# A decoder layer's SwiGLU "down" product in two groups of 4 and 7 chunks instead of three groups

## The chip, the cores and the metric

The kernel runs on one core of one Trainium2 chip. The metric is device time in microseconds (us) of one execution; 1763.42 us is the median of three runs of the kernel before (1762.24 to 1764.12).

## The reference, cut to what matters

One decoder layer for 256 tokens of width 2048, all in float32: a SwiGLU feed-forward block, a token mixer (latent attention and sparse attention side by side), a second SwiGLU block, each followed by a residual sum and a layer norm. Only the two feed-forward blocks are touched:

```
def swiglu(x, w_gate, w_up, w_down):
    return (jax.nn.silu(x @ w_gate) * (x @ w_up)) @ w_down
...
        x = layer_norm(DEEPNORM_ALPHA * x + FFN_RES_WEIGHT * swiglu(x, ffn1_w_gate[l], ffn1_w_up[l], ffn1_w_down[l]),
                       ln1_g[l], ln1_b[l])
...
        x = layer_norm(DEEPNORM_ALPHA * x + FFN_RES_WEIGHT * swiglu(x, ffn2_w_gate[l], ffn2_w_up[l], ffn2_w_down[l]),
                       ln3_g[l], ln3_b[l])
```

`w_gate` and `w_up` are 2048 x 5632, `w_down` is 5632 x 2048. The 5632 hidden columns are 11 *chunks* of 512.

## The kernel before, in words

**Products in three parts.** Each float32 operand is split into a rounded part and a remainder (`split`, L90: a cast on ScalarE, L91, then a subtraction on VectorE, L92), and each block product is three matmuls of 512 columns (`mm3`, L94: L96, L97, L98). L97 is the one that needs the remainder of the weights, `wlo`, which VectorE makes last.

**Units.** `gemm2` (L251) computes two column tiles of 512 (a *column pair*) for both token tiles at once. It walks over *units*: two row tiles of the weight (2 x 128 rows) by two column tiles. An ordinary unit is 8 block products, 24 matmuls, and two loaded buffers to split. A *seven-product unit* (Strassen-Winograd) is 7 block products, 21 matmuls. For it VectorE also forms sums of weights (L318 of 1024 columns, L319 and L320 of 512), and four buffers are split: `a` (1024 columns), `b` (512), and the sums `t13` and `t24` (1024 each). It also needs sums of the left operand, which `trans` (L455) or `sums` (L386) make earlier. While sevens run, four PSUM banks hold outputs and four hold shared products. After the last seven of a column pair the four shared products are combined (ScalarE copy L357, VectorE L358 to L361), and at the end of the pair each of the four output banks gets its combination added (L370) and is handed to `fin`, which for "down" adds it to the residual `y` (L526 for the first group, L528 later). For the last group `done` follows: layer norm statistics of that piece (`ln_stats`, L561), and when a token tile is whole, its layer norm.

**Buffers.** Loaded weights go through 5 buffers (`rawp`), weight sums through 3 (`sump`), the split parts through 6 pairs (`hip`, `lop`). Where a product has no sevens, loads alternate between `rawp` and `sump` by a counter (`new_raw`, L143).

**Order of the work.** TensorE and the DMA queue of SyncE run in program order as written. VectorE and ScalarE instructions are put in an order when the program is built, and that order is fixed: an instruction that stands behind a waiting one is issued after it. Transposes of the hidden activations are generators (`trans`, spawned at L504 and L516) that are stepped by `tick`, each time a given count of products later; `held` keeps them out of the sevens, where all 8 banks are in use.

**The feed-forward block** (`ffn`, L448) goes: gate and up of chunks 0-1 and 2-3, gate 4-5, **down of group 0** (chunks 0 to 3), up 4-5, gate and up 6-7, gate 8-9, **down of group 1** (chunks 4 to 7), up 8-9, gate and up of chunk 10 (`last`, L506), **down of group 2** (chunks 8 to 10). Groups 0 and 1 are 8 units per column pair, 4 of them sevens. Group 2 is 6 units with 2 sevens for the first column pair; the second column pair has no sevens and runs through `gemm` (L177), one column tile after the other, the last with `tail=6`: all products of token tile 0 first, then those of token tile 1, so that the layer norm of tile 0 runs beside tile 1. In all 4+4, 4+4 and 2 sevens: 18 per block.

## Time and profile before

| what | value |
|---|---|
| median of three runs | 1763.42 us (1762.24 to 1764.12) |
| profiled execution, first to last instruction | 1761.7 us |
| TensorE (PE) busy, 8058 matmuls | 1741.7 us, 99% |
| VectorE (DVE) busy | 1596.9 us, 91% |
| ScalarE (ACT) busy | 993.9 us, 56% |
| mean granted TensorE clock | 0.998 |

The profiled execution's own device time is not listed apart from the three runs; its span is 1.7 us below their median.

How to read the profile: a busy time is that of one engine, and engines overlap. The time shown for one matmul (some 390 ns) includes its way through the array, and matmuls overlap in it, so what a matmul costs is the distance from start to start. The same holds in smaller measure on VectorE: the chain of waits, which counts each instant once, gives what an instruction costs behind another one. Ln is line n of the kernel before.

### The profile page before, as it was taken

How to read it: one execution, taken by the hardware profiler on the slowest of the kernel's cores; microseconds unless marked ns; L12 is line 12 of the kernel's file. 1: busy time of each engine (PE TensorE's matmuls, PEld its weight loads, DVE VectorE, ACT ScalarE, POOL GpSimd, SP SyncE). 2: the span in 40 equal slices, each digit the busy share in tenths (PEclk: the TensorE clock that was granted, in tenths of full speed). 3: DMA queues.
4: the chain of work that ended last, by engine and by line, in shares of the span. 5: the costliest groups of instructions: out<-in, count | busy, mean ns of one | idle time of the engine just before them, and what ended most of it. 6: DMA issues, size and time to landing. Idle time of an engine off the chain costs nothing.

```text
span 1761.7 us, 22427 instructions
## 1 busy us (share of the span) xinstructions
PE 1741.7 (99%) x8058; PEld 1429.6 (81%) x8058; DVE 1596.9 (91%) x2123; ACT 993.9 (56%) x1306; POOL 17.0 (1%) x39
## 2 busy tenths in 40 slices
PE   9999999999999999999999999999999999999997
PEld 7888888888888888887788778888888878878886
DVE  7899999999999998765587679999999999999997
ACT  6656555574655565654455556565655565655651
POOL 0000000000000000000000000000000000000000
PEclk9999999999999999999999999999999999999999
DMA  9665666556656657545853355655566556556654
GB/s 334 218 211 178 204 204 203 191 184 212 197 196 225 204 172 255 181 139 206 283 195 111 132 168 179 203 179 203 192 206 222 201 181 215 191 193 217 203 200 159
DMA packets 103408, 350.01 MB, mean 199 GB/s; under 512 B 11136, under 2 KB 13696, under 8 KB 103296
## 3 DMA queue, kind: packets, MB, share of 16 engines
q1 hardware_dynamic: 102016, 344.39, 58.3%
q0 software_dynamic: 1280, 4.20, 0.9%
q8 instruction: 63, 1.03, 0.2%
q14 instruction: 49, 0.40, 0.1%
HBM read 346.44 MB, written 2.10 MB: 198 GB/s over the span
## 4 chain that ended last, share of the span: by engine, by line
PE 78%; DVE 14%; issue 3%; DMA 3%; ACT 2%; SPq 0%; DVEq 0%; POOL 0%; ACTq 0%; POOLq 0%
PE bank L97 24%; PE bank L96 24%; PE bank L98 24%; DVE wlo L92 6%; DVE sum L318 2%; DMA raw<-in_ffn_w_down 1%; DVE w L370 1%; ACT whi L91 1%; DVE sum L320 1%; DVE sum L319 1%; DMA raw<-in_ffn_w_up 1%; PE bank L1022 1%; DVE tlo L471 1%; PE bank L463 1%; PE bank L948 1%
## 5 line engine op out<-in xcount | busy, mean ns | idle before, releaser
L96 PE MATMUL bank<-whi,thi 128*128 128x512 f32 (+1 forms) x1934 | 761.6, 394 | 1.2 <-ACT whi L91 1.2
L97 PE MATMUL bank<-wlo,thi 128*128 128x512 f32 (+1 forms) x1934 | 751.6, 389 | 2.7 <-DVE wlo L92 2.5
L98 PE MATMUL bank<-whi,tlo 128*128 128x512 f32 (+1 forms) x1934 | 751.4, 389 | 0.0
L91 ACT CAST whi<-raw 128x1024 fp32r<-128x1024 f32 (+2 forms) x569 | 533.6, 965 | 272.1 <-PE bank L98 142.0
L92 DVE TENSOR_TENSOR wlo<-raw,whi 128x1024 fp32r<-128x1024 f32 (+2 forms) x569 | 624.8, 1113 | 53.5 <-ACT whi L91 52.6
L91 ACT CAST whi<-sum 128x1024 fp32r<-128x1024 f32 x267 | 278.9, 1050 | 366.4 <-DVE sum L320 140.1
L96 PEld LDWEIGHTS bank<-whi,thi 128*128 128x128 f32 x1934 | 363.2, 188 | 79.3 <-issue 4.1
L97 PEld LDWEIGHTS bank<-wlo,thi 128*128 128x128 f32 x1934 | 363.4, 188 | 75.9 <-DVE wlo L92 4.9
L98 PEld LDWEIGHTS bank<-whi,tlo 128*128 128x128 f32 x1934 | 363.0, 188 | 75.7
L92 DVE TENSOR_TENSOR wlo<-sum,whi 128x1024 fp32r<-128x1024 f32 x267 | 319.6, 1216 | 24.8 <-ACT whi L91 23.2
L97 PE MATMUL bank<-wlo,m 128*128 128x512 f32 x424 | 166.2, 392 | 2.4 <-DVE wlo L92 2.4
L98 PE MATMUL bank<-whi,m 128*128 128x512 f32 x424 | 165.1, 389 | 0.0
L96 PE MATMUL bank<-whi,m 128*128 128x512 f32 x424 | 165.0, 389 | 0.0
L318 DVE TENSOR_TENSOR sum<-raw 128x1024 f32<-128x1024 f32 x106 | 129.3, 1219 | 9.9 <-DMA raw<-in_ffn_w_down 5.4
L97 PEld LDWEIGHTS bank<-wlo,m 128*128 128x128 f32 x424 | 79.6, 188 | 22.6 <-DVE wlo L92 6.1
L96 PEld LDWEIGHTS bank<-whi,m 128*128 128x128 f32 x424 | 79.6, 188 | 16.8
L98 PEld LDWEIGHTS bank<-whi,m 128*128 128x128 f32 x424 | 79.6, 188 | 16.1
L370 DVE TENSOR_TENSOR w<-bank,w 128x512 f32<-128x512 f32 x120 | 79.0, 683 | 0.3
L320 DVE TENSOR_TENSOR sum<-sum,raw 128x512 f32<-128x512 f32 x106 | 72.6, 685 | 0.2
L319 DVE TENSOR_TENSOR sum<-sum,raw 128x512 f32<-128x512 f32 x106 | 72.6, 685 | 0.0
L773 ACT ACTIVATE w<-w,mx 128x256 f32<-128x256 f32 (+1 forms) x48 | 21.4, 446 | 30.4 <-DVE mx L769 27.4
L463 PEld LDWEIGHTS bank<-ident,w 128*128 128x128 f32 x176 | 21.9, 140 | 5.8
(188 smaller groups left out, 944.9 us busy)
## 6 DMA issues: line engine op xcount, KB each, us to landing
raw<-in_ffn_w_down SPq DMA_DIRECT2D x169, 512.0 KB, 4.8
raw<-in_ffn_w_up SPq DMA_DIRECT2D x160, 512.0 KB, 4.7
raw<-in_ffn_w_gate SPq DMA_DIRECT2D x146, 512.0 KB, 4.8
raw<-in_ffn_gu SPq DMA_DIRECT2D x32, 512.0 KB, 4.4
raw<-in_w_in SPq DMA_DIRECT2D x30, 512.0 KB, 4.8
raw<-in_w_out SPq DMA_DIRECT2D x20, 512.0 KB, 3.3
sum<-in_w_in SPq DMA_DIRECT2D x18, 512.0 KB, 5.9
sum<-in_ffn_w_gate SPq DMA_DIRECT2D x12, 512.0 KB, 4.4
```

Source lines behind the costliest of these rows:

```text
L91: A.copy(hi, src)
L92: V.tensor_tensor(lo, src, f(hi), op=OP.subtract)
L96: PE.matmul(ps, xh, wh, start=first, stop=False)
L97: PE.matmul(ps, xh, wl, start=False, stop=False)
L98: PE.matmul(ps, xl, wh, start=False, stop=last)
L318: V.tensor_tensor(t13, a_, b_[:, 1:2, :].broadcast_to([P, 2, NCH]), op=OP.add)
L319: V.tensor_tensor(t24[:, 0], t13[:, 0], a_[:, 1], op=OP.add)
L320: V.tensor_tensor(t24[:, 1], t24[:, 0], b_[:, 0], op=OP.add)
L370: V.tensor_tensor(rest[b], B[b], rest[b], op=OP.add)
L463: PE.transpose(pt[:, j, :], hs[c, t][:, j * P:(j + 1) * P], ident)
L471: V.tensor_tensor(hT[c, t][1], src, f(hT[c, t][0]), op=OP.subtract)
L773: A.activation(s[:, h, :], s[:, h, :], AF.Exp, bias=mx[:, h:h + 1], accum_out=sm[:, h:h + 1])
```

## The change

- Group 0 of "down" (chunks 0 to 3) stays. Groups 1 and 2 become one group of chunks 4 to 10, run after `last`. It has 14 units per column pair, 6 of them sevens, in both column pairs: 4+4 and 6+6, 20 per block.
- The order of its units is a table with a row for each column pair (`REST`); `gemm` is no longer used for "down".
- The transposes of chunks 8 and 9, before spread over `last`, and of chunk 10 are all made at the start of the new group.
- `up` of chunks 8-9 follows `gate` of 8-9 directly and takes the unit order `UP` instead of `LATE`.
- The last three units of the last column pair (`tail=3`) run output bank by output bank: for (token tile, column tile) in (0,0), (0,1), (1,0), (1,1), 18 matmuls each, then that bank's sum and `fin`.

```
+SUMMED = (0, 1, 4, 5, 9)
+REST7 = (8, 9, 10, 11, 18, 19)
+REST = ((12, 13, 14, 15, 8, 9, 16, 10, 11, 17, 18, 20, 19, 21), (12, 8, 9, 13, 10, 11, 14, 18, 19, 15, 16, 17, 20, 21))
...
-    def gemm2(x, xs, kps, seven, w, cp, finish, each=None, head=0, pre=None):
+    def gemm2(x, xs, kps, seven, w, cp, finish, each=None, head=0, pre=None, tail=0):
...
-        for at, (i, ops) in enumerate(todo):
+        for at, (i, ops) in enumerate(todo[:len(todo) - tail]):
...
+        lasts = [(i, ops, weights(at, i)) for at, (i, ops) in list(enumerate(todo))[len(todo) - tail:]]
         for b in [(t, j) for t in range(NT) for j in range(2)]:
+            for i, ops, wt in lasts:
+                for o, (d, xp, name) in enumerate(ops):
+                    if d == b:
+                        mul(i, o, d, xp, name, wt)
+                tick(1)
             if rest:
                 V.tensor_tensor(rest[b], B[b], rest[b], op=OP.add)
             finish(*b, rest.get(b, B[b]))
...
-        groups = [[0, 1, 2, 3], [4, 5, 6, 7], [8, 9, 10]]
...
-            gemm2(x, xs, LATE if c0 in (4, 8) else UP, UP7, name + "_w_up", c0 // 2, fin, each=after if c0 == 0 else None)
-            spawn(trans((c0, c0 + 1), now[0] + DFF, (0, 1, 4, 5, 9)), "T")
+            gemm2(x, xs, LATE if c0 == 4 else UP, UP7, name + "_w_up", c0 // 2, fin, each=after if c0 == 0 else None)
+            if c0 < 8:
+                spawn(trans((c0, c0 + 1), now[0] + DFF, SUMMED), "T")
...
-            spawn(trans((10,), now[0] + DLAST), "T")
+            spawn(trans((8, 9, 10), now[0] + DLAST, SUMMED), "T")
...
-                if gi == 2:
+                if gi:
                     done(t, n)
             for cp in range(2):
-                if gi < 2 or cp == 0:
-                    base = 2 * grp[0]
-                    order, sevens = (DOWN, DOWN7) if gi < 2 else (range(6), (2, 3))
-                    gemm2(xh, hS, [base + i for i in order], [base + i for i in sevens], name + "_w_down", cp,
-                          lambda t, j, r: fin(t, 2 * cp + j, r))
-                    continue
-                for n in (2 * cp, 2 * cp + 1):
-                    gemm(xh, wd, n, ks, lambda t, ps: fin(t, n, ps), tail=6 if n == 3 else 0)
+                order, sevens = (REST[cp], REST7) if gi else (DOWN, DOWN7)
+                gemm2(xh, hS, order, sevens, name + "_w_down", cp, lambda t, j, r: fin(t, 2 * cp + j, r),
+                      tail=3 if gi and cp else 0)
         for step, n in ((gate, 0), (up, 0), (gate, 2), (up, 2), (gate, 4), (down, 0), (up, 4), (gate, 6), (up, 6), (gate, 8),
-                        (down, 1), (up, 8)):
+                        (up, 8)):
             step(n)
         last()
-        down(2)
+        down(1)
```

What this does to VectorE's queue, at two places. The lines of the changed kernel are shifted against those of the one before: L95 is L92 (`wlo`), L321 to L323 are L318 to L320 (weight sums), L361 to L364 are L358 to L361 (combining the shared products), L379 is L370 (output bank plus combination), L534 is L528 (add to `y`), L562 is L561 (statistics), L591 is L590, L555 is L554, L630 and L631 are L629 and L630. `y_92` and `y_93` are token tiles 0 and 1.

First place: the end of the first column pair of the last group, first block. VectorE before, where an ordinary product (`gemm`, no sevens) comes next:

```order
L92 TENSOR_TENSOR wlo<-sum,whi 128x1024
L370 TENSOR_TENSOR w<-bank,w 128x512
L92 TENSOR_TENSOR wlo<-sum,whi 128x1024
L528 TENSOR_TENSOR y_92<-w,y_92 128x512
L370 TENSOR_TENSOR w<-bank,w 128x512
L561 BN_STATS bn_5977<-y_92 128x6
L528 TENSOR_TENSOR y_92<-w,y_92 128x512
```

The splits of the next weights stand between the steps of the finish there. In the changed kernel the same place reads as follows (ahead of it stand L361, L321 and L362; `sum` and the two `wlo<-raw` at the end belong to unit 8, the first seven of the second column pair, which comes after one ordinary unit):

```order
L322 TENSOR_TENSOR sum<-sum,raw 128x512
L363 TENSOR_TENSOR w<-bank,w 128x512
L364 TENSOR_TENSOR w<-bank,w 128x512
L379 TENSOR_TENSOR w<-bank,w 128x512 x2
L534 TENSOR_TENSOR y_92<-w,y_92 128x512 x2
L562 BN_STATS bn_5599<-y_92 128x6 x2
L379 TENSOR_TENSOR w<-bank,w 128x512 x2
L534 TENSOR_TENSOR y_93<-w,y_93 128x512 x2
L562 BN_STATS bn_5606<-y_93 128x6 x2
L323 TENSOR_TENSOR sum<-sum,raw 128x512
L95 TENSOR_TENSOR wlo<-raw,whi 128x1024
L95 TENSOR_TENSOR wlo<-raw,whi 128x512
```

All twelve steps of the finish now stand in one block ahead of the splits for unit 8. The second block's feed-forward has the same rows at this place.

Second place: the end of the program. VectorE before, the last layer norm of token tile 1 (behind the last rows of tile 0's):

```order
L630 SCALAR_TENSOR_TENSOR y_92<-y_92,rstd,w 128x512
L528 TENSOR_TENSOR y_93<-bank,y_93 128x512
L561 BN_STATS bn_15369<-y_93 128x6
L590 BN_AGGR mv<-bn_15369 128x2
L554 TENSOR_SCALAR rstd<-mv 128x1
```

And in the changed kernel:

```order
L631 SCALAR_TENSOR_TENSOR y_92<-y_92,rstd,w 128x512
L379 TENSOR_TENSOR w<-bank,w 128x512 x2
L534 TENSOR_TENSOR y_93<-w,y_93 128x512 x2
L562 BN_STATS bn_14978<-y_93 128x6 x2
L591 BN_AGGR mv<-bn_14978 128x2
L555 TENSOR_SCALAR rstd<-mv 128x1
```

Between the layer norm of tile 0 and the aggregation of tile 1 stand six steps instead of two: both column tiles of tile 1 are finished there.

On TensorE the changed program has 12 matmuls fewer. In the mixer the numbers of matmuls stay, but the counter behind `new_raw` stands elsewhere: the first loads of `w_in` went to `sum` twice, `raw` five times, `sum` once; now they go to `raw` three times, `sum` three times, `raw` twice.

More of the change, by code (lines that the diff above doesn't have):

```diff
@@ L448, in ffn @@
     def ffn(name, x, xs, done, begin=None, after=None, late=()):
-        wg, wu, wd = (W[name + n] + (W2[name + n][0],) for n in ("_w_gate", "_w_up", "_w_down"))
-        groups = [[0, 1, 2, 3], [4, 5, 6, 7], [8, 9, 10]]
         late = list(late)
@@ L515, in last @@
             gemm2(x, xs, GATE, GATE7, name + "_gu", 0, fin)
-            spawn(trans((10,), now[0] + DLAST), "T")
+            spawn(trans((8, 9, 10), now[0] + DLAST, SUMMED), "T")
         def down(gi):
-            grp = groups[gi]
-            ks = list(range(grp[0] * 4, (grp[-1] + 1) * 4))
             xh = lambda k, t: sl(hT[k // 4, t], k % 4)
```

## The prediction

> **What bounds the kernel now.** I read the page first, then the stretches (windows) of the feed-forward blocks, then the chain of waits around the one place where the kernel before already does what the new code does twice, and last the end of the program.
>
> ```profile
> span 1761.7 us, 22427 instructions
> PE 1741.7 (99%) x8058; PEld 1429.6 (81%) x8058; DVE 1596.9 (91%) x2123; ACT 993.9 (56%) x1306; POOL 17.0 (1%) x39
> DVE  7899999999999998765587679999999999999997
> PE 78%; DVE 14%; issue 3%; DMA 3%; ACT 2%; SPq 0%; DVEq 0%; POOL 0%; ACTq 0%; POOLq 0%
> ```
>
> TensorE (PE) is never long idle, and VectorE (DVE) is at nine tenths or more in both feed-forward blocks (slices 3 to 15 and 25 to 39) and looser in the mixer between them. The chain is 78% TensorE and 14% VectorE. The stretches say how close the two are; the columns are the stretch, then busy us and (instructions) of PE, PEld, DVE, ACT, POOL, then the granted clock:
>
> ```profile
> 40.00:120.00 80.00, 80.00 (x355) 66.24 (x354) 69.95 (x77) 45.80 (x51) 0.00 (x0) 1.00 0.65 217
> 290.00:370.00 80.00, 80.00 (x354) 66.23 (x353) 79.86 (x92) 44.99 (x49) 0.00 (x0) 1.00 0.64 211
> ```
>
> Of 354 matmuls one or two lie across the edges, so one costs 80/353 = 0.227 us at full clock. With sevens (290:370) as without (40:120) TensorE issues at that rate, but with sevens VectorE has 0.14 us to spare in 80. So a seven-product unit is worth 3 x 0.227 = 0.68 us to TensorE, and it is free only while VectorE is ahead. An ordinary unit is 24 x 0.227 = 5.44 us, a seven 21 x 0.227 = 4.76 us.
>
> What VectorE's steps cost behind one another, and what happens when they come late, stands in the chain at the switch between the column pairs of the first "down" (start, us, what):
>
> ```profile
> 251.30 6.43 DMA raw<-in_ffn_w_down
> ...
> 257.83 1.23 DVE sum L318
> 259.06 1.13 DVE wlo L92
> 260.19 0.60 DVE sum L319
> 260.79 0.60 DVE wlo L92
> 261.39 1.20 DVE w L370 x2
> 262.59 0.60 DVE y L526
> 263.19 0.60 DVE w L370
> 263.79 1.20 DVE y L526 x2
> 264.99 0.60 DVE w L370
> 265.60 0.60 DVE sum L320
> 266.19 0.60 DVE y L526
> ...
> 269.07 1.13 DVE sum L318
> ...
> 273.14 1.15 DVE wlo L92
> 274.29 0.04 issue
> 274.34 0.50 PE bank L97
> ```
>
> A step over 512 columns costs 0.60, one over 1024 costs 1.14. So a seven-product unit costs VectorE 4 x 1.14 + 3 x 0.60 = 6.36 us against TensorE's 4.76, an ordinary one 2 x 1.14 = 2.28 against 5.44: sevens put VectorE behind, ordinary units let it catch up. Here eight steps of the finish (four L370, four L526) lie among the first seven's splits, and the second seven's third split (`t13`) is late. TensorE shows it:
>
> ```profile
> 273.44 0.40 PE L96 MATMUL bank<-whi,m 128*128 128x512 f32 x1
> 274.34 0.50 PE L97 MATMUL bank<-wlo,m 128*128 128x512 f32 x1 [0.50 <-DVE wlo L92]
> ```
>
> Start to start that is 0.90 in place of 0.23: 0.7 us lost. This place has two ordinary units after the last seven, and one ahead of the next two.
>
> **The change part by part.**
>
> *Matmuls.* Two sevens more in each block: 2 x 2 x 3 = 12 matmuls fewer, 12 x 0.227 = **-2.7 us**. No cover is needed, since TensorE is the engine on the chain.
>
> *VectorE's total.* One finish less in each block (four combinations L358 to L361, four L370, eight additions to `y`): 32 steps in all, 32 x 0.60 = 19.2 us less. Four sevens more: 4 x (6.36 - 2.28) = 16.3 us more. The total hardly moves; what counts is where it lies.
>
> *The two middle downs go, and `up` of 8-9 follows `gate` of 8-9.* In the old group 1 TensorE waited once, in the second block:
>
> ```profile
> PE bank L97 <- DVE wlo L92: 0.6, 1, 0.6
> ```
>
> That view counts from a matmul's modelled end, so start to start the loss is somewhat more, and smaller ones fall under it: **-1.0 us** (-0.5 to -1.7). What takes its place is a switch like that of chunks 6-7, without transposes that need sums; I put it at nothing, and at 0.8 us if VectorE isn't ahead there.
>
> *Transposes of chunks 8 to 10.* The same 24 in six groups, now all in the first four units of the new group. These are ordinary ones, 4 x 5.44 = 21.8 us of TensorE against 4 x 2.28 = 9.1 us of VectorE, so the transposes' splits and sums (six steps of 0.60 and some 3 us for chunk 9) have 12 us of cover. The first seven behind them is not late: **0**. In VectorE's queue the weights of units 15, 8 and 9 stand behind these transposes; without that cover each would cost a step, under 1 us.
>
> *The first column pair* has 6 sevens in the last ten units, with ordinary ones between: from the first to the last, 6 x 6.36 + 3 x 2.28 = 45.0 us of VectorE against 6 x 4.76 + 3 x 5.44 = 44.9 us. Even, and VectorE starts ahead: **0**.
>
> *The switch to the second column pair.* This is the term that decides. Count from the moment at which TensorE ends unit 19, the last seven. TensorE has two ordinary units before the next seven, 21 and 12: unit 8 begins at 10.9. VectorE can't be far ahead: the six pairs of split buffers hold unit 19's four and unit 21's two, and unit 12's must wait until unit 19 gives its first ones back, some 3 us before its end, and for ScalarE, whose casts take about 1 us each and which copies L357 first. I take unit 12's splits as done at 0.3. Then, in the order printed above: four combinations 2.4, the weight sums L318 and L319 1.7, twelve steps of the finish 12 x 0.60 = 7.2 (here four are statistics, L561, which the first "down" lacks), L320 0.6, and the first split of unit 8, 1.14: done at 0.3 + 13.0 = 13.3. TensorE needs it at 10.9 + 0.23 = 11.1 and stops for **2.2 us**. Then unit 8's other splits and unit 9's steps up to its third split follow: 13.3 + 0.60 + 2 x 1.14 + (6.36 - 1.14) = 21.4, and TensorE without a delay wants that at its tenth matmul of unit 9, 10.9 + 4.76 + 10 x 0.227 = 17.9. So by there **3.5 us** are lost; the waits don't fall exactly on one another, which I allow with 0.4. After that come ordinary units between pairs of sevens, and VectorE keeps up. I take **3.9 us for each block, 7.8 in all**. The late step is of the same kind as the one at 274.34, where the loss was 0.7. Bounds: 2.0 each if unit 12's splits are done 2 us earlier; 5.5 each if loads arrive late as in the row at 251.30, where VectorE waited for a transfer of 6.43.
>
> *The end of the program.*
>
> ```profile
> 1743.38 0.69 DVE L528 TENSOR_TENSOR y<-bank,y 128x512 f32<-128x512 f32 x1 [5.05 <-PE bank L98]
> 1744.11 0.69 DVE L561 BATCH_NORM_STATS2 bn<-y 128x6 f32<-128x512 f32 x1
> 1749.84 0.75 DVE L630 SCALAR_TENSOR_TENSOR y<-y,rstd,w 128x512 f32<-128x512 f32 x1
> 1751.54 0.69 DVE L528 TENSOR_TENSOR y<-bank,y 128x512 f32<-128x512 f32 x1 [0.95 <-PE bank L98]
> 1752.26 0.69 DVE L561 BATCH_NORM_STATS2 bn<-y 128x6 f32<-128x512 f32 x1
> 1752.99 0.26 DVE L590 BATCH_NORM_AGGREGATE mv<-bn 128x2 f32<-128x24 f32 x1
> ```
>
> Token tile 1 again has 36 matmuls after tile 0 ends (8.16 us between the two L528). Tile 0's work on VectorE begins with one step more (L370 ahead of L528, 0.72 as from L528 to L561), so its last step, now at 1749.84, starts at 1750.56 and gives way at 1751.2, when tile 1's last matmuls are just done. Now six steps stand there instead of two: 1751.2 + 5 x 0.60 + 0.73 = 1754.9 for L590, which was at 1752.99. **+1.9 us**, all exposed. Bounds: 0.7 (the one step more), 2.5.
>
> *From the first block into the mixer.* The same extra step, and the last three units give back their split buffers only in the last quarter of the tail (18 matmuls, 4.1 us), where the old tail gave one back every 6 matmuls from its middle on. Six of the first eight pieces of `w_in` are split some 4 us later. Waits there now:
>
> ```profile
> PE bank L98 <- DVE tlo L92: 0.3, 1, 0.3
> PE bank L96 <- ACT thi L91: 0.3, 1, 0.3
> ```
>
> Both are of the layer norm's first transposed piece, which now stands behind one step more: **+0.4 us** (0 to 2.0, if the weights become the later of the two).
>
> *The mixer* keeps its instructions, but loads take other buffers. VectorE has slack there (digits 5 to 8 in slices 16 to 24), so 0, with 1.5 us to either side.
>
> Sum: -2.7 - 1.0 + 7.8 + 1.9 + 0.4 = **+6.4 us**. The profiled span of 1761.7 becomes 1768.1; the median lies 1.7 above that span, and with the same 1.7 it becomes 1769.8, say 1769.8.
>
> The Trainium skill, "Perfetto Trace Analysis", section "Identifying the Most-Contended Engine", has it that the engine with the highest occupancy is the one to improve first; the next section adds that regimes may differ within a kernel. By the first rule alone TensorE, at 99%, decides, and the whole change is the 2.7 us of matmuls: 1760.7. The rows of 290:370 and 274.34 go against that in these stretches, since there VectorE decides when it is a step late.
>
> **The rivals.** (A measurement of this kernel tells about 0.2%, 3.5 us, from no change: faster is below 1759.9, slower above 1766.9.)
>
> 1. *The matmuls decide, and the switch is hidden.* VectorE gets far enough ahead in the five-ordinary start and the even middle that unit 8 finds its splits. For it: in 290:370 TensorE loses nothing though VectorE is full. Against it: six pairs of buffers can't hold more than one seven and an ordinary unit. If the end is also hidden: 1763.4 - 2.7 - 1.0 = 1759.7. It decides if the twelve steps end before 9.9 on the count above. Chance 0.05.
> 2. *The switch costs as much as today's.* The loss is 0.7 to 1.5 per block, because the first splits come before the finish in effect or VectorE is 2 to 3 us further ahead. With the end's 1.9: 1763.4 - 3.7 + 2.2 + 1.9 + 0.4 = 1764.2, no change that can be told. For it: the first "down" loses only 0.7. Against it: there the finish has four steps less (2.4 us) and one ordinary unit more (5.44 - 2.28 = 3.2 us). Chance 0.22.
> 3. *Late weights behind the first block.* Beside the switch, the pieces of `w_in` come late, and the other buffers of the mixer cost a transfer here and there: 3 to 5 us more, 1773 to 1775. For it: six splits in 12 us together with the layer norm's steps. Against it: TensorE needs these pieces one by one, each 6 matmuls after the last. Chance 0.08.
>
> That the change doesn't do what it says I leave out: the order of instructions shows 12 matmuls fewer, in these units.
>
> **How the numbers follow.** The forecast, 1769.8, has 0.65; its own range is 1766.0 (switch 2.0 each, 3.8 less) to 1774.0 (switch 5.5 each, 3.2 more, mixer 1.0 more). For 8 in 10 the range takes in part of rival 2 and most of rival 3's lower end: 1764.0 to 1774.0. Slower by over 0.2%: 0.65 + 0.08 = 0.73. Same: 0.22. Faster: 0.05.
>
> **What would show it.** In the profile of the changed kernel: 8046 matmuls; in each last "down", some 76 us after its start, a wait of TensorE for `wlo` of 1.5 to 3 us where unit 8 begins, right after the block of twelve steps on VectorE, and one or two shorter ones within the next 10 us; the aggregation of token tile 1 some 3.4 us after TensorE releases it, in place of the 1.45 from 1751.54 to 1752.99. The prediction is wrong if TensorE has no wait over 1 us at that switch, if the time is below 1764, or if the loss lies elsewhere (the first four units with the transposes, the first pieces of `w_in`, or the mixer).

## The result, and the profile after

The changed kernel takes **1773.93 us** (median of five runs, 1771.41 to 1774.43) against 1763.42 (1761.86 to 1765.60): the ratio is 1.0054, with a 95% interval of 1.0042 to 1.0067. It is slower by about half a per cent. Its profiled execution took 1771.41 us with a span of 1769.7, so it is one of the shorter ones: 8.0 us above the span of before, where the medians differ by 10.5.

The page of the changed kernel, in the lines that answer to those shown of before (span; busy time, share and instructions of each engine; VectorE's busy tenths in 40 slices):

```profile
span 1769.7 us, 22421 instructions
PE 1742.1 (98%) x8046; PEld 1429.0 (81%) x8046; DVE 1596.2 (90%) x2111; ACT 997.0 (56%) x1312; POOL 17.4 (1%) x39
DVE  7899999999998999865587679999999999998998
```

The totals say almost nothing: 12 matmuls and 12 VectorE steps fewer, and the same shares. The waits say where the time went. Here are TensorE's waits, view by view: the switch between the column pairs in the first block (615 to 660) and in the second (1670 to 1710), and the start of the mixer (700 to 720); the columns are what waited, for what, us in total, times, longest.

```profile
PE bank L100 <- DVE wlo L95: 2.2, 1, 2.2
...
PE bank L100 <- DVE wlo L95: 2.8, 2, 2.2
...
PE bank L572 <- DVE y L603: 1.1, 1, 1.1
PE bank L99 <- ACT thi L94: 1.0, 1, 1.0
```

Before, the first two stretches had no wait at all and the third had two of 0.3.

**The switch, seen from both engines.** VectorE in the first block:

```profile
620.56 1.23 DVE L95 TENSOR_TENSOR wlo<-raw,whi 128x1024 fp32r<-128x1024 f32 x1 [1.50 <-ACT whi L94]
621.99 2.36 DVE L95 TENSOR_TENSOR wlo<-raw,whi 128x1024 fp32r<-128x1024 f32 x2 [0.20 <-ACT whi L94]
624.26 0.68 DVE L361 TENSOR_TENSOR w<-bank,w 128x512 f32<-128x512 f32 x1
...
628.40 1.28 DVE L379 TENSOR_TENSOR w<-bank,w 128x512 f32<-128x512 f32 x2
...
634.38 1.28 DVE L562 BATCH_NORM_STATS2 bn<-y 128x6 f32<-128x512 f32 x2
635.57 0.68 DVE L323 TENSOR_TENSOR sum<-sum,raw 128x512 f32<-128x512 f32 x1
636.16 1.82 DVE L95 TENSOR_TENSOR wlo<-raw,whi 128x1024 fp32r<-128x1024 f32 x2
```

TensorE at the same place; the matmul of 634.87 is the first of unit 8, the next one the first that needs its `wlo`:

```profile
634.87 0.39 PE L99 MATMUL bank<-whi,thi 128*128 128x512 f32 x1
637.44 0.50 PE L100 MATMUL bank<-wlo,thi 128*128 128x512 f32 x1 [2.18 <-DVE wlo L95]
```

ScalarE, whose casts these splits wait for:

```profile
619.47 1.05 ACT L94 CAST whi<-raw 128x1024 fp32r<-128x1024 f32 x1 [1.67 <-PE bank L101]
```

VectorE waits for casts, and the casts wait for split buffers that TensorE gives back: ScalarE stood idle 1.67 us ahead of this cast and 1.66 ahead of the one before it, each time until a matmul of L101 was done. So buffers limit VectorE's lead here, as the prediction had it, and not loads. VectorE then works without a gap from 621.99 on; the twelve steps of the finish fill 628.40 to 635.57; unit 8's first split starts at 636.16; and TensorE stands from 634.87 to 637.44. That is 2.57 start to start, 2.34 more than the usual 0.23. The second block loses the same (1685.87 to 1688.44).

**The end of the program.** VectorE, behind tile 0's last step, and TensorE's last matmul (the second fence is TensorE's last matmul of before):

```profile
1756.48 0.75 DVE L631 SCALAR_TENSOR_TENSOR y<-y,rstd,w 128x512 f32<-128x512 f32 x1
1757.14 1.29 DVE L379 TENSOR_TENSOR w<-bank,w 128x512 f32<-128x512 f32 x2
1758.34 1.29 DVE L534 TENSOR_TENSOR y<-w,y 128x512 f32<-128x512 f32 x2
1759.54 1.28 DVE L562 BATCH_NORM_STATS2 bn<-y 128x6 f32<-128x512 f32 x2
1760.86 0.27 DVE L591 BATCH_NORM_AGGREGATE mv<-bn 128x2 f32<-128x24 f32 x1
...
1757.03 0.39 PE L101 MATMUL bank<-whi,tlo 128*128 128x512 f32 x1
```

```profile
1751.11 0.39 PE L98 MATMUL bank<-whi,tlo 128*128 128x512 f32 x1
```

All six steps lie behind the last matmul: the aggregation starts 3.83 us after that matmul, where it was 1.88 before (1752.99, in the prediction's rows, less 1751.11).

**The sum.** I took, for each matmul, what its distance to the next start exceeds the usual distance of its kind, and added this by stretch, for the profiled executions of before and after. Around each group of transposes one distance is 0.09 us longer and the one ahead of it 0.08 shorter, with no wait in the view. At the switch and in the middle downs, where the two programs have different numbers of such groups, I leave these out; at the start of the mixer both have seven, 0.6 us in each of the two figures:

| part | predicted, us | measured, us |
|---|---|---|
| 12 matmuls fewer | -2.7 | -2.7 |
| middle downs (second block; before 1.4, after 0) | -1.0 | -1.4 |
| switch, both blocks (before 0 and 0, after 4.02 and 3.77) | +7.8 | +7.8 |
| the two tails, last three units (0; 0.86 and 0.72) | 0 | +1.6 |
| start of the mixer (1.70; 3.56) | +0.4 | +1.9 |
| end of the program (1.88; 3.83) | +1.9 | +1.95 |
| everything else | 0 | -1.2 |
| sum | +6.4 | +7.9 |

The spans differ by 8.0. "Everything else" is program text that is the same in both. It is not steady from one execution to another: the same sum over the first 575 us, which no edit of the experiments below touches, was some 7 us in this profile and between 6 and 10.5 in the twelve others. This is why single spans are read by stretch here, and the medians carry the verdicts.

### The profile page after: what moved, and what is told of

It reads as the page before. It is cut to its first block, busy times and chain, and to the rows that moved or that the text cites. A ratio compares the mean times of both kernels' runs of the same rounds, so it can differ in the third digit from the quotient of the medians.

```text
span 1769.7 us, 22421 instructions
## 1 busy us (share of the span) xinstructions
PE 1742.1 (98%) x8046; PEld 1429.0 (81%) x8046; DVE 1596.2 (90%) x2111; ACT 997.0 (56%) x1312; POOL 17.4 (1%) x39
## 5 line engine op out<-in xcount | busy, mean ns | idle before, releaser
L101 PE MATMUL bank<-whi,tlo 128*128 128x512 f32 (+1 forms) x1914 | 744.2, 389 | 0.0
L94 ACT CAST whi<-raw 128x1024 fp32r<-128x1024 f32 (+1 forms) x577 | 539.5, 963 | 273.4 <-PE bank L101 130.5
L95 DVE TENSOR_TENSOR wlo<-raw,whi 128x1024 fp32r<-128x1024 f32 (+1 forms) x577 | 632.8, 1111 | 66.0 <-ACT whi L94 65.5
L94 ACT CAST whi<-sum 128x1024 fp32r<-128x1024 f32 (+1 forms) x267 | 278.5, 1049 | 376.0 <-DVE sum L323 156.8
L101 PEld LDWEIGHTS bank<-whi,tlo 128*128 128x128 f32 x1914 | 359.7, 188 | 74.6
L95 DVE TENSOR_TENSOR wlo<-sum,whi 128x1024 fp32r<-128x1024 f32 (+1 forms) x267 | 319.9, 1216 | 36.8 <-ACT whi L94 34.5
L100 PE MATMUL bank<-wlo,m 128*128 128x512 f32 x440 | 172.6, 392 | 1.8 <-DVE wlo L95 1.8
L99 PE MATMUL bank<-whi,m 128*128 128x512 f32 x440 | 171.8, 390 | 0.0
L101 PE MATMUL bank<-whi,m 128*128 128x512 f32 x440 | 171.6, 390 | 0.0
L321 DVE TENSOR_TENSOR sum<-raw 128x1024 f32<-128x1024 f32 x110 | 134.1, 1219 | 5.0 <-DMA raw<-in_ffn_w_up 4.6
L99 PEld LDWEIGHTS bank<-whi,m 128*128 128x128 f32 x440 | 82.9, 188 | 17.4
L101 PEld LDWEIGHTS bank<-whi,m 128*128 128x128 f32 x440 | 82.9, 188 | 16.9
L379 DVE TENSOR_TENSOR w<-bank,w 128x512 f32<-128x512 f32 x112 | 73.2, 683 | 5.6 <-PE bank L101 5.5
L323 DVE TENSOR_TENSOR sum<-sum,raw 128x512 f32<-128x512 f32 x110 | 75.4, 685 | 0.2
L470 PEld LDWEIGHTS bank<-ident,w 128*128 128x128 f32 x176 | 21.9, 140 | 5.8
```

The costliest lines, as they stand in the source:

```text
L94: A.copy(hi, src)
L95: V.tensor_tensor(lo, src, f(hi), op=OP.subtract)
L99: PE.matmul(ps, xh, wh, start=first, stop=False)
L100: PE.matmul(ps, xh, wl, start=False, stop=False)
L101: PE.matmul(ps, xl, wh, start=False, stop=last)
L321: V.tensor_tensor(t13, a_, b_[:, 1:2, :].broadcast_to([P, 2, NCH]), op=OP.add)
```

## The experiments

Theory A: at the switch, VectorE's queue decides, the block of twelve steps and the lead with which VectorE arrives there; the rest of the loss is the end and VectorE's queue at the start of the mixer. Theory B: VectorE is only the last link, and late loads or casts decide. The kernels below are the changed one with the edit shown, unless another base is named.

### The changed kernel again

> The changed kernel once more, unaltered, for the comparison with the three beside it on the same chip: 1773.9 (1771.4 to 1774.5), with waits of 2.3 to 2.5 us at the two switches. If the spread of its runs comes from the slow matmuls behind such a wait (1.8 us where they follow, as in the first block of its first profile, and none in the second), a profile with 1774 shows them behind both waits or behind another, and one with 1771.5 behind one or none.

Measured: 1773.01 (1771.62 to 1773.96), ratio to before 1.0054 (1.0040 to 1.0068). The switch lost 3.79 and 3.76 us, and no slow matmuls followed either wait. So slow matmuls behind the switch are not what separates the runs: the first profile had them in the first block and still lost only 4.02 there. The matmuls ran slower, VectorE caught up meanwhile, and the second wait (0.25 and 0.76 in the other places) didn't come. My price of 1.8 us for them in the expectations below was wrong: net they cost 0.2 to 0.3.

### Four statistics out of the switch

```
+            def first_stats(at):
+                for t in range(NT):
+                    if at in (9, 10):
+                        ln_stats(t, at - 9)
...
-                if gi:
+                if gi and cp:
                     done(t, n)
```

> The changed kernel, with the four statistics (L562) of the first column pair of the last down taken out of the finish at the switch and put behind units 15 and 16 of the second pair (the scheduler puts one of them ahead of unit 9's last split, one among the four combinations). Theory A (VectorE's block of twelve steps decides when unit 8's first split is done): the block is 4 x 0.60 = 2.4 us shorter, so TensorE's first wait at the switch goes from 2.45 us (start to start over a matmul's own 0.23) to about 0.1 in both blocks, the sum of the switch from 3.7 (second block, 2.45 + 0.36 + 0.88) to about 1.3, and in the first block the slow matmuls behind the wait (0.43 us start to start for eight of them, 1.8 us) go too. About 5 us in all from 1773.9: 1769 (1768 to 1770.5). Theory B (the wait is for the cast or the load of unit 8's weights, and VectorE only stands last in the chain): the wait stays at 2 us or more, 1773 to 1774.5.

Measured: 1770.25 (1769.14 to 1771.74), ratio 1.0032 (1.0020 to 1.0044). The 2.2 is gone from both blocks; what is left at the switch is, in each block:

```profile
PE bank L100 <- DVE wlo L95: 0.6, 1, 0.6
```

Start to start the switch lost 1.8 in each block, 2.0 to 2.2 less than in the changed kernel (I had expected 1.3 to be left). Four steps of 0.60 are 2.4; one of them had come back ahead of unit 9's last split. No load or cast was touched. Theory B falls here.

### Two ordinary units ahead of the first seven of the second pair

```
-REST = (..., (12, 8, 9, 13, 10, 11, 14, 18, 19, 15, 16, 17, 20, 21))
+REST = (..., (12, 13, 8, 9, 14, 10, 11, 15, 18, 19, 16, 17, 20, 21))
```

> The changed kernel, with two ordinary units ahead of the first seven of the second column pair in place of one (12, 13, 8, 9, 14, 10, 11, 15, 18, 19, 16, 17, 20, 21): the same units, but one ordinary unit is taken from between the last seven and the tail. Theory A: unit 8 is wanted one ordinary unit later, by which VectorE gains 5.44 - 2.28 = 3.2 us, so the sum of the switch goes from 3.7 to about 0.5 in each block and the slow matmuls of the first block go: 6.4 to 8.2 us less. Whether it is given back shows what the waits of the tail are (now 0.86 and 0.73 us): if they come from VectorE being late, they grow by up to 3 us a block with one unit less to catch up (1768 to 1772 in all); if they come from the tail's three units holding all six pairs of split buffers, they stay, and the time is 1766 to 1767.5. Theory B (loads or casts): the switch keeps 2 us or more.

Measured: 1768.73 (1766.82 to 1770.94), ratio 1.0025 (1.0016 to 1.0034). The switch lost 0.52 and 0.51, as expected from 3.2 us more lead. The tails lost 1.00 and 1.00, hardly more than before, with one ordinary unit less to catch up in. For tails that stay as they were I had expected 1766 to 1767.5, so the time is over a microsecond too high for that. In its profile the first 575 us, which the edit doesn't reach, lost some 2.8 us more than in the profile of after.

### Three ordinary units behind the last seven of the first pair

```
-REST = ((12, 13, 14, 15, 8, 9, 16, 10, 11, 17, 18, 20, 19, 21), ...)
+REST = ((12, 13, 14, 8, 9, 15, 10, 11, 16, 18, 19, 17, 20, 21), ...)
```

> The changed kernel, with the first column pair's sevens drawn ahead, so that three ordinary units stand behind the last seven in place of one (12, 13, 14, 8, 9, 15, 10, 11, 16, 18, 19, 17, 20, 21); the second pair is as it was. The twelve steps and the sevens are the same in number; only VectorE's lead is changed. Theory A: the sums are done and VectorE is ahead as far as its buffers allow when the finish comes, and the finish itself, with two ordinary units in front of it, starts at the same place: the four combinations (2.4 us) and the sums of the weights come earlier, so the first wait goes from 2.45 to about 0 to 0.5 and the switch from 3.7 to at most 1.2; slow matmuls gone. 1773.9 - 2 x 2.5 - 1.8 = 1767 (1765.5 to 1769), unless the first seven, one unit earlier behind the transposes, is late (up to 1 us a block). Theory B: no change at the switch.

Measured: 1772.66 (1771.17 to 1775.42), ratio 1.0042 (1.0025 to 1.0059). The switch lost nothing in either block, but the time hardly fell, since another wait took its place. TensorE in the first block, then VectorE:

```profile
621.85 0.60 PE L470 MATMUL bank<-ident,w 128*128 128x128 f32 x4
...
623.63 0.50 PE L99 MATMUL bank<-whi,thi 128*128 128x512 f32 x1 [0.48 <-ACT thi L477]
...
626.32 0.50 PE L101 MATMUL bank<-whi,tlo 128*128 128x512 f32 x1 [1.95 <-DVE tlo L478]
```

```profile
622.38 1.22 DVE L95 TENSOR_TENSOR wlo<-raw,whi 128x1024 fp32r<-128x1024 f32 x1
624.44 1.22 DVE L321 TENSOR_TENSOR sum<-raw 128x1024 f32<-128x1024 f32 x1 [0.84 <-DMA raw<-in_ffn_w_down]
625.58 0.68 DVE L478 TENSOR_TENSOR tlo<-bank,thi 128x512 fp32r<-128x512 f32 x1
```

L470 is a transpose of a hidden chunk and L478 its remainder. `held` keeps transposes out of the sevens; with one ordinary unit fewer at the front, the last ones were made only behind the last seven, right before the units that need them, and L478 stands in VectorE's queue behind a weight sum that waits for its load. My expectation (1767) had allowed 1 us a block for that; it was 2.8 (0.65 and 2.12), in both blocks. In the first block TensorE also ran at half rate behind it (granted clock 0.52 over 627.0 to 630.5), some 1.5 us more.

### Two ordinary units behind the last seven

```
-REST = ((12, 13, 14, 15, 8, 9, 16, 10, 11, 17, 18, 20, 19, 21), ...)
+REST = ((12, 13, 14, 15, 8, 9, 16, 10, 11, 17, 18, 19, 20, 21), ...)
```

> The changed kernel, with units 19 and 20 of the first column pair of the last down exchanged (..., 10, 11, 17, 18, 19, 20, 21), so that two ordinary units stand behind its last seven in place of one; the first four units, in which the transposes of chunks 8 to 10 run, are as they were, and so is the second pair. It repeats the question of the order with three ordinary units behind the last seven, where the switch was free of waits but the transposes of the last chunk, held until the last seven was done, stopped TensorE for 2.9 us. Theory A (VectorE's lead): one ordinary unit more is 3.2 us of lead, the first wait of 2.45 goes to 0 to 0.3 and the switch from 3.7 to 0.5 to 1.0, without the transposes' wait: 1773.9 less 2 x 3 and less the slow matmuls of one block 1.8: 1766 to 1769. Rival (the lead is limited by loads: before the block of twelve steps VectorE was idle for 2.9 us, while the casts waited for transfers): the unit more is not used, and 1.5 us or more of wait stays in each block: 1770.5 to 1772.

Measured: **1765.23** (1763.55 to 1768.37), ratio 1.0012 (1.0003 to 1.0021). Two numbers of the table exchanged give back most of the loss. The switch lost 0.99 and 0.97. The first wait is gone, the one at unit 9 stays. The rival of a lead limited by loads falls: the unit more was used. Here is the lead in numbers: an ordinary unit more ahead of unit 8 is 3.2 us of VectorE's time, and the switch fell by 2.8 to 3.0 in each block. The span of its profile, 1763.5, is 6.2 below the changed kernel's: the switches and tails account for 6.7, and 0.5 was lost in stretches that no edit touches.

### The combination added to y before the tail

`early` adds a combination to its piece of `y`; the bank is then added by `fin` alone, so each output of the tail has one step less behind its matmuls.

```
+            if early and at == s_at[-1] + 1:
+                for b in rest:
+                    early(*b, rest[b])
...
-            finish(*b, rest.get(b, B[b]))
+            finish(*b, B[b] if early else rest.get(b, B[b]))
```

> The changed kernel, with the combined products of the second column pair of the last down added to y behind unit 15, before the tail, so that in the tail each output tile costs VectorE two steps (L534, L562) in place of three (L379, L534, L562); no step is added or left out but that the addition of the bank to the combination becomes an addition to y. The switch is untouched. Theory A (the end is six VectorE steps behind tile 0's eight): tile 0 gives way a step earlier and four steps stand in place of six, so the aggregation of token tile 1 comes 1.9 us nearer to the last matmul (now 1760.86 against 1757.03: 3.8 behind its start, then about 1.9 to 2.5); the layer norm into the mixer gains 0.6 to 1.2 of its 1.9. 1773.9 - 2.5 = 1771.4 (1770.3 to 1772.3). Rival: the end hangs on the matmuls or on the last aggregation and stores, and nothing changes: 1773.5 to 1774.

Measured: 1775.63 (1774.99 to 1777.06), ratio 1.0063 (1.0048 to 1.0078): no gain over the changed kernel (1.0054), and above both of the times that I had expected. The end did what the theory said. VectorE, with the last matmul at 1762.34:

```profile
1761.72 0.68 DVE L537 TENSOR_TENSOR y<-bank,y 128x512 f32<-128x512 f32 x1
...
1764.48 0.27 DVE L598 BATCH_NORM_AGGREGATE mv<-bn 128x2 f32<-128x24 f32 x1
```

That is 2.14 from the last matmul to the aggregation in place of 3.83, 1.7 gained. But the four additions stand ahead of unit 16's splits, VectorE first, then TensorE:

```profile
683.38 1.88 DVE L543 TENSOR_TENSOR y<-w,y 128x512 f32<-128x512 f32 x3
685.19 5.76 DVE L95 TENSOR_TENSOR wlo<-raw,whi 128x1024 fp32r<-128x1024 f32 x5
```

```profile
686.46 0.50 PE L100 MATMUL bank<-wlo,thi 128*128 128x512 f32 x1 [0.91 <-DVE wlo L95]
```

That wait, 1.07 start to start, comes in both blocks and takes more than the end gives. At the start of the mixer the two waits of 1.14 and 1.27 became 1.92 and 0.34: no gain in sum.

### The same for token tile 1 alone

```
+            if early and b == (0, 0):
+                for j in range(2):
+                    early(1, j, rest[1, j])
```

> The changed kernel, with the combined products of token tile 1 alone, of the second column pair of the last down, added to y ahead of the tail's last split, where VectorE was idle for about 2 us, in place of in the finish: tile 1's finish is four steps in place of six. (With all four additions directly behind unit 15 the end was 1.7 us shorter, but the splits of unit 16 came 1.1 us late in both blocks and the mixer's start 0.8.) If what went wrong there was the place of the additions: the end is 1.2 us shorter, the wait at unit 16 doesn't come, the tail's own wait grows by at most 0.5: 1773.9 - 1.2 + 0 to 1.0 = 1772.7 to 1773.7. Rival (any step of VectorE ahead of the tail delays the tail by itself): tail waits 1.2 longer in each block, 1774 to 1775.5.

Measured: 1771.97 (1768.65 to 1772.76), ratio 1.0045 (1.0031 to 1.0059), a little below what I had expected. The end took 2.62, a gain of 1.2 as expected, and unit 16 didn't wait. The two additions stand ahead of the tail's last split. In the first block VectorE was still idle 1.28 us behind them, and that tail lost hardly more than before. In the second block the idle time, 1.60 us, lay one split earlier: the additions put off the last split by their 1.2 us, and that tail grew from 0.7 or 0.9 to 1.55. The start of the mixer lost 4.5 in place of 3.6; TensorE ran at half rate in it (granted clock 0.50 over 710.6 to 713.4), which by itself is some 1.4 us.

### Lead on both sides of the switch, and tile 1's additions

```
+REST = ((12, 13, 14, 15, 8, 9, 16, 10, 11, 17, 18, 19, 20, 21), (12, 13, 8, 9, 14, 10, 11, 15, 18, 19, 16, 17, 20, 21))
...
+            if early and b == (0, 0):
```

> The changed kernel with two ordinary units behind the last seven of the first pair, two ahead of the first seven of the second pair, and the additions of token tile 1 moved as in the run beside this. Theory A: the switch has no waits left in either block; with two ahead in the second pair alone 1768.7 was measured with 0.5 left per block, so 1768.7 - 1.0 - 0 to 1.2 = 1767 (1765.5 to 1768.5), not below the kernel before (1764.1 on this chip), since the tail's late loads (about 1.0 per block), the start of the mixer (1.5) and the rest of the end are not touched. Rival: below 1764, the change's matmuls then come through.

Measured: 1766.78 (1763.29 to 1768.62), ratio 1.0016 (1.0007 to 1.0025). The switch lost nothing, in both blocks: with 6.3 us more lead even unit 9 is on time. It isn't faster than with one unit alone, since the first block's tail lost 1.6 and the mixer's start 4.7 (with a half-rate stretch, granted clock 0.50 over 712 to 715), and its profile lost some 10.5 us in the first 575, which no edit reaches, where the profile of after lost some 7.

### Tile 1's half of the tail unit by unit

```
-                    if d == b:
-                        mul(i, o, d, xp, name, wt)
+                    if d == b or b == (1, 0) and d == (1, 1):
+                        if b != (1, 1):
+                            mul(i, o, d, xp, name, wt)
```

> The kernel with two ordinary units behind the last seven of the first pair (1765.2 on its own run), with token tile 1's half of the tail unit by unit in place of output by output: 12 matmuls of unit 17, then of 20, then of 21, both outputs done at the very end. At the end of the program VectorE is busy with tile 0 until the last matmul anyway, so nothing changes there (3.8 us from the last matmul's start to the last aggregation). At the start of the mixer the two theories part: if TensorE's 1.14 us wait there comes from the split buffers, which the tail gives back only in its last quarter, the first two pairs come back 12 matmuls into tile 1's half in place of 24, 2.7 us earlier, and that wait falls to 0.4 as in the kernel before; if it comes from token tile 1's steps on VectorE among tile 0's layer norm, it also changes, but the 1.27 us wait of tile 1's transposes grows, since all six steps now come after the last matmul (up to 3 us). 1764.4 by the first, 1765.2 to 1767 by the second.

Measured: 1769.09 (1767.31 to 1774.30), ratio 1.0038 (1.0026 to 1.0049), 4 us slower than its base, the kernel with two ordinary units behind the last seven, and above the 1767 that I had allowed. The end stayed at 3.83. At the start of the mixer both waits grew, TensorE first, then VectorE and ScalarE:

```profile
706.55 0.50 PE L99 MATMUL bank<-m,thi 128*128 128x512 f32 x1 [2.90 <-ACT thi L94]
715.69 1.12 PE L573 MATMUL bank<-ident,y 128*128 128x128 f32 x4 [2.66 <-DVE y L604]
```

```profile
701.14 2.36 DVE L95 TENSOR_TENSOR wlo<-sum,whi 128x1024 fp32r<-128x1024 f32 x2 [0.48 <-ACT whi L94]
703.41 0.69 DVE L380 TENSOR_TENSOR w<-bank,w 128x512 f32<-128x512 f32 x1
704.01 0.40 DVE L582 TENSOR_SCALAR w<-bank,pack 128x128 f32<-128x128 f32 x1
...
705.88 0.62 ACT L94 CAST thi<-w 128x512 fp32r<-128x512 f32 x1
```

The buffers did come back earlier, and the splits of `w_in` did start earlier. They now stand ahead of tile 0's first layer-norm step (L582 here), whose result TensorE waits for. So the wait is not one for weights: it is tile 0's normalized piece, queued on VectorE behind whatever weight splits and tile 1 steps come first. Of the two theories of that run the first falls; by the second, the wait of tile 1's transposes grew from 1.27 to 2.82 (up to 3 was allowed), but I hadn't seen that the first wait would grow too, to 3.06. Behind the second wait TensorE ran at half rate as well (granted clock 0.50 over 715.7 to 718.6).

### The additions on GpSimd, alone and with the tail by units

Both also start from the kernel with two ordinary units behind the last seven; the second has the tail of the last section as well.

```
-                V.tensor_tensor(yc, r, yc, op=OP.add)
+                G.tensor_tensor(yc, r, yc, op=OP.add)
```

> The kernel with two ordinary units behind the last seven of the first pair (1765.2 on its own run), with the combined products of the second pair added to y behind unit 15 by GpSimd in place of by VectorE in the finish: each output of the tail costs VectorE two steps in place of three, and none is put ahead of the splits. With the same additions on VectorE the end was 1.7 us shorter but the splits of unit 16 came 1.1 us late in each block. If that was the place in VectorE's queue, the end is 1.7 shorter here and no wait comes at unit 16: 1765.2 - 1.7 - 0 to 1.2 at the start of the mixer = 1763 (1762 to 1764), even with the kernel before. Rivals: GpSimd's additions are so slow that the finish waits for them (no row of these traces shows such an addition; from unit 15 to the first finish there are some 11 us for four), or VectorE's steps stretch while GpSimd works: 1765 to 1768.

> Both edits of the two runs beside this together. If both work: 1765.2 - 1.7 - 0.8 and up to 1.0 less at the tile 1 transposes: 1762.5 (1761 to 1764), a little below the kernel before (1763.5 on this chip) or even with it. If either fails alone it shows here by the same waits.

Measured: `pool_adds` 1765.37 (1762.97 to 1768.00), ratio 1.0006 (0.9997 to 1.0015), no longer distinguishable from before; `unit_pool` 1767.66 (1764.51 to 1769.94), ratio 1.0020 (1.0011 to 1.0030). The end took 2.22 in the first, a gain of 1.6, and unit 16 didn't wait. But the median didn't fall below that of its base (1765.23): 1763 was expected, and 1765 to 1768 by the rival in which VectorE's steps stretch while GpSimd works. That rival's sign is in the trace: two splits that took 2.36 together in the kernel of after took 4.56 beside the additions, in each block. TensorE hardly waited for it there: the tails lost 0.7 and 0.6. The mixer's start again lost 3.6, with 1.92 in place of 1.14 and 1.27. With the tail by units it lost 5.4 (half rate over 710.3 to 713.3), and 1762.5 was expected.

### What helped, together

```
+REST = ((12, 13, 14, 15, 8, 9, 16, 10, 11, 17, 18, 19, 20, 21), (12, 13, 8, 9, 14, 10, 11, 15, 18, 19, 16, 17, 20, 21))
...
+                G.tensor_tensor(yc, r, yc, op=OP.add)
...
+                      tail=3 if gi and cp else 0, early=early if gi and cp and name == "ffn2" else None)
```

> The changed kernel with what helped before: two ordinary units behind the last seven of the first pair, two ahead of the first seven of the second pair, and GpSimd's additions in the second block alone (in the first block they only exchanged the two waits of the mixer's start, 1.92 for 1.14 and 1.27). From 1765.2 with the first edit alone: the switch's remaining 1.0 in each block goes, the end is 1.6 shorter, the tails' waits grow by 0.3 to 1.0 in each block, as they did with two units ahead: 1765.2 - 2.0 - 1.6 + 1.3 = 1762.9 (1761.5 to 1764.5), even with the kernel before (1763.0 on the last chip) or a little below it, since the start of the mixer (1.9 more than before) and the rest of the end (0.3) still stand against the 3.7 that the matmuls and the middle downs give. Rival: VectorE has no slack left in the second pair's last units, and the tails take back what the switch gives: 1764.5 to 1766.

Measured: 1769.01 (1766.79 to 1774.23) against 1765.33 for the kernel before on that chip, ratio 1.0022 (1.0013 to 1.0031). That is above the 1762.9 expected and above the rival's 1764.5 to 1766 too. What the rival names happened: the switch lost nothing and the end took 2.22, but the second tail lost 6.4 (and the first 2.1). GpSimd and VectorE there (GpSimd's two rows share the addition that begins at 1740.36; the first row's other one ran from 1738.24):

```profile
1738.24 4.46 POOL L543 TENSOR_TENSOR y<-w,y 128x512 f32<-128x512 f32 x2 [1.83 <-DVE w L362]
...
1740.36 4.57 POOL L543 TENSOR_TENSOR y<-w,y 128x512 f32<-128x512 f32 x2
```

```profile
1739.16 0.68 DVE L363 TENSOR_TENSOR w<-bank,w 128x512 f32<-128x512 f32 x1
...
1740.36 1.21 DVE L95 TENSOR_TENSOR wlo<-raw,whi 128x1024 fp32r<-128x1024 f32 x1
...
1741.49 4.53 DVE L95 TENSOR_TENSOR wlo<-raw,whi 128x1024 fp32r<-128x1024 f32 x2
```

Two splits that take 2.36 elsewhere took 4.53 beside GpSimd's two additions, and TensorE waited for both:

```profile
PE bank L100 <- DVE wlo L95: 2.7, 3, 1.3
```

These waits are 3.2 us start to start; most of the rest of the 6.4 is a half-rate stretch behind them (granted clock 0.50 over 1745.7 to 1752.0). The profile is also the slowest of the eleven executions, 5.2 us above their median, and 5.5 us of what it lost more than the profile of after lie between 1100 and 1480, where no edit reaches. What the tail loses in an execution near the median isn't known.

No version measured here beats the kernel before. The best, with the exchange of two units, is 0.12% above it, and with GpSimd's additions 0.06%, which isn't resolved.

## Why the prediction was right

The time, 1773.9, lies on the side to which I gave 0.73, some 4 us above the number and only 0.1 below the upper end of the range, with some of the runs above it. I had set that end for late loads at the switch, and they didn't come. The mechanism was right; that the time still fell inside the range is partly luck, since other terms were too small. By its steps:

- **The switch** decided, at the place and by the mechanism given. The count from the end of unit 19 can be laid on the trace: unit 8 began at 634.87 and two ordinary units lie between, so unit 19 ended at 634.87 - 10.9 = 623.97. Unit 12's splits were done at 624.26, 0.3 later (taken: 0.3), the twelve steps ended at 635.57, 11.6 (taken: 0.3 + 2.4 + 1.7 + 7.2 = 11.6), and unit 8's first split was done at 636.16 + 1.14 = 637.30, 13.3 (taken: 13.3). The first wait was 2.34 (taken: 2.2), the whole switch 3.8 to 4.0 (taken: 3.9). Removing four of the steps, or putting an ordinary unit on either side, took from it about what the count says (2.0 to 2.2 of 2.4, and 2.8 to 3.0 of 3.2 with the unit behind the last seven).
- **Rival 1** (matmuls decide) fails: TensorE's 12 matmuls are gone and the time rose. The prediction also read the rule of occupancy too simply. The section of the Trainium skill that it names there ("Perfetto Trace Analysis", "Identifying the Most-Contended Engine") doesn't judge TensorE by its matmuls' busy time, 99% here, but by its useful work against the peak and by the share of its weight loads. By that share, 81%, it stands below VectorE's 91%. **Rival 2** (a switch as cheap as the first "down") holds only where the order gives the lead: with two ordinary units behind the last seven the switch cost 1.0 and the time was 1765.2, near its 1764.2.
- **The end** was right in mechanism and size: 1.95 for 1.9. Taking two or four steps out of it gave 1.2 and 1.7.
- **The start of the mixer** was under-sized, 1.9 for 0.4, inside its bounds of 0 to 2.0. I had rival 3 with late weights in mind. The experiment that returns the buffers earlier made it worse, so the late piece is the layer norm's. Why it is late is read from the rows and not separated by a run: a column tile of token tile 1, three steps that stood elsewhere before, and the `w_in` splits, now later, come between tile 0's steps in VectorE's queue. The rows of after, VectorE first, then ScalarE:

```profile
702.92 0.68 DVE L379 TENSOR_TENSOR w<-bank,w 128x512 f32<-128x512 f32 x1
703.64 0.69 DVE L534 TENSOR_TENSOR y<-w,y 128x512 f32<-128x512 f32 x1
704.37 0.69 DVE L562 BATCH_NORM_STATS2 bn<-y 128x6 f32<-128x512 f32 x1
704.98 0.40 DVE L581 TENSOR_SCALAR w<-bank,pack 128x128 f32<-128x128 f32 x1
```

```profile
705.79 1.99 ACT L94 CAST whi<-sum 128x1024 fp32r<-128x1024 f32 x2
707.68 0.80 ACT L579 ACTIVATE w<-bank,pack 128x128 f32<-128x128 f32 x2
```

  The two engines make the quarters of a piece by turns, and ScalarE comes to the last quarter of the first piece (707.68) only behind two casts of `w_in`, where before one stood at that place.

- **The tails** had no term in the prediction; they cost 0.9 and 0.7 in this profile, 0 and 0.9 in the second one of the same kernel. The cast of the last unit waits for its transfer, as ScalarE's row shows:

```profile
1740.75 1.05 ACT L94 CAST whi<-raw 128x1024 fp32r<-128x1024 f32 x1 [2.25 <-DMA raw<-in_ffn_w_down]
```

  That the load's own time makes the difference is argued from this row and from the tail that came and went in one and the same code; no run separated it.
- **Transposes, first column pair, matmuls, mixer**: as predicted, within 0.2 us. The middle downs gave 1.4 in place of 1.0, inside their bounds. The transposes do need those four ordinary units, but not only as cover for VectorE: with three there was no room for the last ones ahead of the sevens, they were made behind the last seven, and 2.8 us were lost there.
- The rest of the 4 us between 1769.8 and 1773.9 is the profiled execution's place among the runs: I had put the median 1.7 above its span, and this span's run was the shortest of five, 2.5 below the median.

## What to carry to other kernels

Where two engines are evenly loaded, price a new order of work at the place where the loads change hands: count both queues from one common event up to the next thing that is wanted, since the totals (TensorE 99%, VectorE 91%) don't tell. A block of steps that comes all at once needs its cover on one side or the other, and exchanging two units in the order (about 8 us here) is worth more than 12 matmuls (2.7 us). A step moved to an idle place is only free if the order that is built puts it there and nothing is held up by it: the additions taken out of the finish shortened the end each time, by 1.2 to 1.7 us, and in two kernels cost more than that elsewhere.

## What the runs showed of the hardware

**The clock halves after a wait of 2.3 us, sometimes.** The stretches of after, before the wait, in the slow matmuls behind it, and then (us; busy us and instructions of PE, PEld, DVE, ACT, POOL; granted clock, DMA share, GB/s):

```profile
600.00:634.00 34.00, 34.00 (x152) 28.15 (x151) 31.03 (x38) 16.65 (x19) 0.00 (x0) 1.00 0.57 189
638.70:641.90 3.20, 3.20 (x9) 2.55 (x8) 3.20 (x4) 0.57 (x2) 0.00 (x0) 0.50 0.83 289
642.00:646.00 4.00, 4.00 (x18) 3.22 (x17) 3.94 (x6) 2.11 (x3) 0.00 (x0) 0.98 0.48 133
```

From 638.70 eight matmuls lie 0.43 apart in place of 0.23, and then the clock is back. Of eight such waits at the switch (two in each profile of this kernel, and two in each of the two kernels of the additions that left the switch alone) two were followed by it. The Trainium skill, "TensorE: Matmul & The Clock Gate", Part 1, has the clock at half after an idle window of about 3.4 us, with windows that run freely. The half rate lasted that long here (8 x 0.43 = 3.4 us), but it followed losses of 2.3 us. It followed smaller ones too: in `first_ends_three`, `both_two` and `combined` a loss of 1.6 us and one of 0.3 within 2.5 us behind it (granted clock 0.50 over 398.5 to 401.5, 398.0 to 401.0 and 1448.5 to 1451.7). Between 20 us and the last matmul, every half-rate stretch in the fourteen profiles comes behind waits that cost 1.4 us or more, so the wait is taken for its cause; no run changed a wait alone to show it.

**GpSimd blocks VectorE's splits.** The Trainium skill, "SBUF — State Buffer", section "Who interferes with whom", says that a VectorE instruction with two inputs in SBUF contends with a GpSimd instruction that reads SBUF, and calls the ports that they share an exclusive lock. The rows of 1740.36 and 1741.49 agree: two splits (each with two inputs in SBUF) took 4.53 beside two GpSimd additions of 4.57 (and 4.56 in each block of `pool_adds`), as if they ran by turns, while VectorE's step at 1739.16, which has one input in a PSUM bank, kept its 0.68 beside the addition that began at 1738.24.
